# Hybrid decoder block on one core: a new layout of the query columns of the scan's small levels, value columns computed in pairs, meta products in other steps, and one more turn per head

## The chip, the cores and the metric

The kernel runs on one core of a Trainium2 chip. The metric is the device time of one execution in microseconds (us); less is better. Before the change the median of three runs is 873.73 us (872.95 to 874.18).

The engines in the profile: PE is TensorE (matrix products; PEld is its loading of the stationary operand), DVE is VectorE, ACT is ScalarE, POOL is GpSimd, and SP is SyncE, which issues the transfers from device memory (HBM).

## The reference

One layer over 16 meta tokens followed by 512 real tokens, model width 1024, all in float32. Cut to what matters:

```python
u = rmsnorm(h, attn_norm_w)
q, f_raw, i_in, g_out, b_gate, c_gate, x_conv, gate_a, gate_b = split(u @ w_in)   # nine times 1024 columns
q = silu(q);  f = lb + (1 - lb) * sigmoid(f_raw);  k = 1 - f;  v = i_in
o = hgrn2(q, k, v, log f)      # 8 heads of 128: S_t = diag(f_t) S_{t-1} + k_t v_t^T,  o_t = S_t^T q_t
y_a = rmsnorm(o per head) * silu(g_out)
y_b = b_gate * causal_conv3(c_gate * x_conv)
h = h + (sigmoid(gate_a) * y_a + sigmoid(gate_b) * y_b) @ w_out
a, val = split(rmsnorm(h) @ w_up);  h = h + (silu(causal_conv3(a) + b) * val) @ w_down
return rmsnorm(h)[:, 16:]
```

## The kernel before

**Stages.** (1) 0 to about 40 us: loading, the first norm, and the first columns of the input projection (forget gate, query and value of head 0). (2) About 40 to 460 us, called the scan stage here: the rest of the input projection, 128 columns at a time, and between its matmuls the recurrence of the eight heads, one after the other. (3) About 460 to 580 us: output projection and the first six blocks of the FFN. (4) The rest of the FFN and the last norm. The change lies in stage (2).

**Projection.** A float32 product is made of three matmuls in a split format: each operand is cast to a short upper part on ACT, and the lower part is what DVE subtracts from it (L100 and L101 for a single unit, L303 and L304 for a pair). A *single unit* gives one block of 128 output columns for all 528 positions: 8 blocks of the contraction, 3 matmuls each, for each half of the positions, 48 matmuls of 264 columns (`half_unit`, L452). A *pair* gives two such blocks with seven products in place of eight (`Pair`, L343, with `product`, L322): the weights' quarters are first added up on DVE (L313, L314, L318), every product is 4 blocks times 3 matmuls (L330 to L332), and the results are put together from PSUM by a *sink*, a class with four small methods (`FQ`, `CX`, `GA`, `BG`) on DVE and ACT, while ACT copies partial results out (`keep`, L336). A pair loads 1.5 MB of weights (`pair_weights`, L288), a single 0.5 MB. Forget gate with query, conv gate with conv input, output gate with gate a, and b gate with gate b go in pairs; from head 1 on the values are singles, copied by ACT into one tile `V_t` (`value`, L764). The list `items` (L869) gives the order: for each head j the pair FQ of head j+1, the value unit of head j+1, then CX, GA and BG of head j, then the merge.

**Recurrence of a head** (`recur`, L490). It is a generator, and each `yield` ends a step. `tick` (L108) is called after every two contraction blocks of a product; each `beat[1]`-th tick resumes the generator once, so that its small matmuls stand between the large ones. Steps: value transposes; three levels (`LEVELS`: m of 1, 4 and 16 positions in groups of g = 32, 32 and 64); the level of 64; key transposes; state products; output products (L620, L621) with the row norm's statistics; and the last, transposes of the normalised rows (L633) and of the meta rows `om` (L635). What is not done at the head's end is flushed in `merge` (L774). The beat is 6, and 4 for the last head.

**A level** takes blocks of four sub-blocks of m positions. For the sub-blocks of queries that look back on the keys, it lays out six columns' worth of queries in `qv` (L536 to L540), ordered by how many sub-blocks lie between; ACT makes one copy, DVE three products with the decays `T`. Small matmuls of 32 or 64 stationary columns (L544) give the scores in PSUM, DVE then scales the queries in place in three products (L546 to L548) and the keys in one (L556), and three masked copies (L562) put the scores where they belong, by a mask that the host makes.

**Meta products.** Keys of the meta tokens times two queries (L573, 16 stationary columns) stand in the level of 64, in front of its matmuls of 64 stationary columns (L578). Their weighted sum with the values (L611, 2 stationary columns) stands in the step of the state products (L602, L604).

**Order.** Each engine works through its own instructions in a fixed order. That order is made beforehand by a planner that goes by the written order as a priority and by its own estimates of when an operand will be ready; so instructions can stand earlier or later than written. DVE's first products for the next head's level stand far ahead of that head's matmuls in this way.

Of the kernel before, what the change touches and what calls it, by code (L numbers as in the profile page):

```python
# [14 lines left out]
P = 128  # L15
D = 1024
KT = D // P
# [23 lines left out]
SINGLE = [("f", 1), ("q", 1), ("i", 1)] + [u for j in range(1, KT) for u in ([("i", j + 1)] if j + 1 < KT else [])]  # L41
PAIRS = [("g", "ga", 0)]
for _j in range(1, KT):
    PAIRS += ([("f", "q", _j + 1)] if _j + 1 < KT else []) + [("c", "x", _j), ("g", "ga", _j), ("b", "gb", _j)]
# [13 lines left out]
def block_kernel(ctx: ExitStack, tc: tile.TileContext, xT, par, wts, pairs, ident, masks, finw, out):  # L58
# [200 lines left out]
    Vms, Kms, oms = ([const.tile([P, P], F32, name=f"{n}{i}") for i in range(2)] for n in ("Vm", "Km", "om"))  # L259
    ams = [const.tile([P, 2], F32, name=f"am{i}") for i in range(2)]  # L260
# [161 lines left out]
    V_t = p1.tile([P, L + 1], F32, name="V")  # L422
# [6 lines left out]
    nc.gpsimd.memset(V_t[:, L:], 0.0)  # L429
    for i in range(2):  # L430
        nc.gpsimd.memset(Ks[i][:, L:], 0.0)
        nc.gpsimd.memset(Fs[i][:, L:], 1.0)
        nc.gpsimd.memset(As[i], 0.0)
# [28 lines left out]
    with tc.tile_pool(name="rp0", bufs=1) as rp:  # L462
# [22 lines left out]
        raw_unit((h3rd, l3rd), lambda o, at: act.copy(V_t[:, at], o))  # L485
# [4 lines left out]
    def recur(j, oS):  # L490
        b = j % 2
        K, V, F, Q, A = Ks[b], V_t, Fs[b], Qs[b][:, T0:], As[b]
# [27 lines left out]
        for lev, (m, g) in enumerate(LEVELS):  # L520
            ng = SEQ // g
            nb = g // (4 * m)
            lo1, lo2, lo3 = 3 * g // 4, 5 * g // 4, 3 * g // 2
            qv = p2.tile([P, NCH * QW], F32, name="qv", tag="qv").rearrange("p (n w) -> p n w", n=ng)
            q4 = Qm.rearrange("p (n b x) -> p n b x", n=ng, x=4 * m)
            k4 = Km_.rearrange("p (b s m) -> p b s m", s=4, m=m)
            t4 = T.rearrange("p (n b s) -> p n b s", n=ng, s=4)
            tf = T.rearrange("p (b s) -> p b s", s=4)
            v1 = qv[:, :, :lo1].rearrange("p n (b x) -> p n b x", x=3 * m)
            v2 = qv[:, :, lo1:lo2].rearrange("p n (b x) -> p n b x", x=2 * m)  # L530
            v3 = qv[:, :, lo2:].rearrange("p n (b x) -> p n b x", x=m)

            def tb(i):
                return t4[:, :, :, i:i + 1].to_broadcast([P, ng, nb, m])

            act.copy(v1, q4[:, :, :, m:])  # L536
            for i in range(2):
                dve.tensor_tensor(v2[:, :, :, i * m:(i + 1) * m], q4[:, :, :, (2 + i) * m:(3 + i) * m],
                                  tb(1 + i), op=ALU.mult)
            dve.tensor_tensor(v3, v2[:, :, :, m:], tb(1), op=ALU.mult)  # L540
            ps = quarter()
            for n in range(ng):
                r = n * g % P
                pe.matmul(ps[r:r + g, n * g // P, :lo3], K[:, M1 + n * g:M1 + (n + 1) * g], qv[:, n, :],  # L544
                          start=True, stop=True, tile_position=(0, r))
            dve.tensor_tensor(q4[:, :, :, m:2 * m], q4[:, :, :, m:2 * m], tb(0), op=ALU.mult)  # L546
            dve.tensor_tensor(q4[:, :, :, 2 * m:3 * m], v2[:, :, :, :m], tb(0), op=ALU.mult)
            dve.tensor_tensor(q4[:, :, :, 3 * m:], v3, tb(0), op=ALU.mult)  # L548
            n4 = SEQ // (4 * m)
# [7 lines left out]
                              op=ALU.mult)  # L557
            B = Bs[g]
            a4 = B.rearrange("p c (b x) -> p c b x", x=4 * m)
            for r, lo_, hi_ in ((3, 0, lo1), (2, lo1, lo2), (1, lo2, lo3)):  # L560
                mk = mk_t[:, lev, lo_:hi_].rearrange("p (b x) -> p b x", x=r * m)
                dve.copy_predicated(a4[:, :, :, (4 - r) * m:],  # L562
                                    mk.unsqueeze(1).to_broadcast([P, NCH, nb, r * m]),
# [200 lines left out]
    def value(j):  # L764
        return lambda o, at: act.copy(V_t[:, at], o)
# [420 lines left out]
```

## Time and profile before

| | us |
|---|---|
| median of 3 runs | 873.73 |
| the profiled execution | 872.9 |
| its span, first to last instruction | 871.1 |
| TensorE busy | 859.1 (99%) |
| VectorE busy | 717.5 (82%) |
| ScalarE busy | 529.3 (61%) |
| GpSimd busy | 37.5 (4%) |
| granted TensorE clock, mean | 0.998 |

Matmuls overlap in TensorE's pipeline, so the time of one row is longer than the distance between two starts. A line number is that of the kernel before. "Idle before" is how long the engine had nothing to run just ahead of an instruction, with what released it.

### The profile page before, as it was taken

The page shows a single profiled execution, that of the slowest core. Times are in us where ns is not written, and L with a number is a line of the kernel's source. Part 1 is how long each engine was busy: PE and PEld are TensorE (multiplying, and loading weights), DVE is VectorE, ACT ScalarE, POOL GpSimd, SP SyncE. Part 2 cuts the span into 40 slices and gives each one's busy share as a digit, 9 for nine tenths or more (in the row PEclk, how much of TensorE's full clock was granted, in tenths as well). Part 3 has the DMA queues.
Part 4 walks back from the last instruction along what each step waited for, and adds up shares of the span by engine and source line. Part 5 has one row for each costly group of instructions (what it writes and reads, how often), then busy time and mean ns, then how long its engine had stood idle before and what let it go on. Part 6 is the DMA issues. An engine that isn't in the chain of part 4 may idle for free.

```text
span 871.1 us, 17481 instructions
## 1 busy us (share of the span) xinstructions
PE 859.1 (99%) x6996; PEld 814.5 (93%) x6996; DVE 717.5 (82%) x1323; ACT 529.3 (61%) x1004; POOL 37.5 (4%) x110
## 2 busy tenths in 40 slices
PE   8999999999999999999999999999999999999996
PEld 8999999999999999999999999999999999999985
DVE  7899999988989889889986559975877777777766
ACT  7847768676676767776684345554554545545434
POOL 1210110100101001020000000000000000000000
PEclk9999999999999999999999999999999999999999
DMA  7216444343343434434234323533443534433302
GB/s 258 98 50 189 137 142 140 98 147 121 122 146 98 146 109 134 136 102 145 81 112 158 98 73 97 169 100 119 144 147 100 173 116 131 160 97 122 121 25 97
DMA packets 38817, 107.98 MB, mean 124 GB/s; under 512 B 4304, under 2 KB 5712, under 8 KB 38736
## 3 DMA queue, kind: packets, MB, share of 16 engines
q1 hardware_dynamic: 38448, 106.34, 38.4%
q8 instruction: 55, 0.90, 0.4%
q10 hardware_dynamic: 288, 0.52, 0.2%
q14 instruction: 26, 0.21, 0.1%
HBM read 104.75 MB, written 2.10 MB: 123 GB/s over the span
## 4 chain that ended last, share of the span: by engine, by line
PE 80%; DVE 12%; ACT 4%; DMA 3%; issue 1%; SPq 0%; DVEq 0%; ACTq 0%
PE pr L330 14%; PE pr L331 13%; PE pr L332 13%; PE psm L123 4%; PE psm L120 4%; PE psm L121 4%; PE psm L1048 4%; PE psm L1047 4%; PE psm L1046 4%; PE pr L437 3%; DVE wl L304 3%; PE pr L438 3%; PE pr L439 3%; DMA wt<-in_pairs 2%; PE psq L544 1%
## 5 line engine op out<-in xcount | busy, mean ns | idle before, releaser
L330 PE MATMUL pr<-cm,wh 128*128 128x264 f32 (+1 forms) x784 | 227.5, 292 | 0.4 <-ACT c L338 0.2
L331 PE MATMUL pr<-cm,wh 128*128 128x264 f32 (+1 forms) x784 | 222.5, 284 | 0.0
L332 PE MATMUL pr<-cm,wl 128*128 128x264 f32 (+1 forms) x784 | 222.5, 284 | 0.0
L330 PEld LDWEIGHTS pr<-cm,wh 128*128 128x128 f32 x784 | 147.4, 188 | 4.7 <-issue 1.3
L332 PEld LDWEIGHTS pr<-cm,wl 128*128 128x128 f32 x784 | 147.8, 189 | 0.1
L331 PEld LDWEIGHTS pr<-cm,wh 128*128 128x128 f32 x784 | 147.5, 188 | 0.0
L303 ACT CAST wh<-wt 128x1024 fp32r<-128x1024 f32 x88 | 92.2, 1053 | 74.3 <-PE psm L1048 33.9
L304 DVE TENSOR_TENSOR wl<-wt,wh 128x1024 fp32r<-128x1024 f32 x88 | 107.0, 1218 | 30.8 <-ACT wh L303 30.5
L100 ACT CAST wh<-wr 128x1024 fp32r<-128x1024 f32 (+1 forms) x64 | 61.7, 968 | 66.7 <-PE psm L121 31.1
L101 DVE TENSOR_TENSOR wl<-wr,wh 128x1024 fp32r<-128x1024 f32 (+1 forms) x64 | 71.6, 1121 | 37.1 <-ACT wh L100 35.8
L330 PE MATMUL pr<-cf,wh 128*128 128x258 f32 x256 | 72.5, 283 | 0.0
L331 PE MATMUL pr<-cf,wh 128*128 128x258 f32 x256 | 72.1, 282 | 0.0
L332 PE MATMUL pr<-cf,wl 128*128 128x258 f32 x256 | 71.9, 281 | 0.0
L338 ACT COPY c<-pr 128x264 f32<-128x264 f32 (+1 forms) x132 | 49.5, 375 | 33.2 <-PE pr L332 25.8
L304 DVE TENSOR_TENSOR wl<-wr,wh 128x1024 fp32r<-128x1024 f32 x44 | 53.7, 1221 | 11.4 <-ACT wh L303 11.2
L303 ACT CAST wh<-wr 128x1024 fp32r<-128x1024 f32 x44 | 46.2, 1049 | 21.6 <-PE pr L331 19.8
L313 DVE TENSOR_TENSOR wt<-wt 128x1024 f32<-128x1024 f32 x44 | 53.6, 1219 | 3.4 <-DMA wt<-in_pairs 3.3
L330 PE MATMUL pr<-cb,wh 128*128 128x258 f32 x192 | 54.7, 285 | 0.3 <-ACT xr L1007 0.3
L331 PE MATMUL pr<-cb,wh 128*128 128x258 f32 x192 | 54.7, 285 | 0.0
L332 PE MATMUL pr<-cb,wl 128*128 128x258 f32 x192 | 54.4, 283 | 0.0
L331 PEld LDWEIGHTS pr<-cf,wh 128*128 128x128 f32 x256 | 48.6, 190 | 0.8
L330 PEld LDWEIGHTS pr<-cf,wh 128*128 128x128 f32 x256 | 48.1, 188 | 0.7
(304 smaller groups left out, 2247.9 us busy)
## 6 DMA issues: line engine op xcount, KB each, us to landing
wr<-in_wts SPq DMA_DIRECT2D x56, 512.0 KB, 3.7
wr<-in_pairs SPq DMA_DIRECT2D x44, 512.0 KB, 4.2
wt<-in_pairs SPq DMA_DIRECT2D x44, 512.0 KB, 4.0
wt<-in_pairs SPq DMA_DIRECT2D x88, 256.0 KB, 4.8
xt<-in_xT SPq DMA_DIRECT2D x8, 264.0 KB, 4.5
xr<-in_xT SPq DMA_DIRECT2D x8, 264.0 KB, 3.8
out<-zf SPq DMA_DIRECT2D x8, 256.0 KB, 2.3
wr<-in_wts SPq DMA_DIRECT2D x8, 128.0 KB, 4.1
```

Source lines behind the costliest of these rows:

```text
L100: act.copy(h[:, i:i + n, :], raw[:, i:i + n, :])
L101: dve.tensor_tensor(lo[:, i:i + n, :], raw[:, i:i + n, :], h[:, i:i + n, :].bitcast(F32), op=ALU.subtract)
L120: pe.matmul(o, wh, rh[:, a:b], start=first, stop=False)
L121: pe.matmul(o, wh, rl[:, a:b], start=False, stop=False)
L123: pe.matmul(o, wl, rh[:, a:b], start=False, stop=last)
L303: act.copy(h, src)
L304: dve.tensor_tensor(lo, src, h.bitcast(F32), op=ALU.subtract)
L313: dve.tensor_tensor(t[:, 1:3, :], t[:, 1:3, :], t[:, 3:, :].to_broadcast([P, 2, 512]), op=ALU.add)
L330: pe.matmul(ps, h[:, j], ch, start=start and j == 0, stop=False, skip_group_check=True)
L331: pe.matmul(ps, h[:, j], cl, start=False, stop=False, skip_group_check=True)
L332: pe.matmul(ps, lo[:, j], ch, start=False, stop=j == 3, skip_group_check=True)
L338: act.copy(c, r)
```

## The change

- The three `qv` parts get a new order: for each block of four sub-blocks, the six columns of m queries stand together. ACT makes two copies, DVE two products in the place of three. The three that scale the queries in place become one, which reads the first three of the six. The masked copies read runs of 3, 2 and 1 sub-blocks out of each six, and the mask is made accordingly.
- The key products of the meta tokens move into the level with m = 4, behind its matmuls of 32 stationary columns. Their sum gets 64 stationary columns and moves into the level of 64, behind that level's matmuls; ACT's two small operations on its result go with it.
- The values of heads 2 and 3, 4 and 5, 6 and 7 are computed as pairs by a new sink `II`, placed behind FQ of heads 2, 4 and 6; the value tile is doubled. Two small tiles (`Km`, `om`) are no longer doubled.
- One more `yield` in front of the last step, and beats of 6, 5 and 4 (head after an even one, after an odd one, last).

```diff
+    if _j + 1 < KT:
+        PAIRS += [(("f", _j + 1), ("q", _j + 1))]
+        if _j % 2:
+            PAIRS += [(("i", _j + 1), ("i", _j + 2))]
...
+    ams = [const.tile([P, 64], F32, name=f"am{i}") for i in range(2)]
...
-            act.copy(v1, q4[:, :, :, m:])
-            for i in range(2):
-                dve.tensor_tensor(v2[:, :, :, i * m:(i + 1) * m], q4[:, :, :, (2 + i) * m:(3 + i) * m],
-                                  tb(1 + i), op=ALU.mult)
-            dve.tensor_tensor(v3, v2[:, :, :, m:], tb(1), op=ALU.mult)
+            act.copy(qs[:, :, 0], q4[:, :, 1])
+            act.copy(qs[:, :, 3::2], q4[:, :, 2:])
+            dve.tensor_tensor(qs[:, :, 1:5:3], q4[:, :, 2:], tf[:, :, 1:3].unsqueeze(3).to_broadcast([P, n4, 2, m]),
+                              op=ALU.mult)
+            dve.tensor_tensor(qs[:, :, 2], qs[:, :, 4], tf[:, :, 1:2].to_broadcast([P, n4, m]), op=ALU.mult)
...
-            dve.tensor_tensor(q4[:, :, :, m:2 * m], q4[:, :, :, m:2 * m], tb(0), op=ALU.mult)
-            dve.tensor_tensor(q4[:, :, :, 2 * m:3 * m], v2[:, :, :, :m], tb(0), op=ALU.mult)
-            dve.tensor_tensor(q4[:, :, :, 3 * m:], v3, tb(0), op=ALU.mult)
+            dve.tensor_tensor(q4[:, :, 1:], qs[:, :, :3], tf[:, :, :1].unsqueeze(3).to_broadcast([P, n4, 3, m]),
+                              op=ALU.mult)
...
+            if m == 4:
+                pma = pmisc.tile([P, 512], F32, name="pm", tag="pm")
+                for i in range(2):
+                    pe.matmul(pma[:16, 2 * i:2 * i + 2], KM[:, i, :], Q[:, 14 - T0:16 - T0], start=True, stop=True)
+                am = ams[b]
+                act.copy(am[:16, :2], pma[:16, 0:4:3])
...
+            for k, a, e in ((0, 0, 3 * m), (1, 3 * m, 5 * m), (2, 5 * m, 6 * m)):
+                dve.copy_predicated(a4[:, :, :, (k + 1) * m:],
+                                    mk[:, :, a:e].unsqueeze(1).to_broadcast([P, NCH, nb, e - a]), got[:, :, :, a:e])
...
-        pma = pmisc.tile([P, 512], F32, name="pm", tag="pm")
-        for i in range(2):
-            pe.matmul(pma[:16, 2 * i:2 * i + 2], KM[:, i, :], Q[:, 14 - T0:16 - T0], start=True, stop=True)
...
+        pms = pmisc.tile([P, 512], F32, name="pm", tag="pm")
+        pe.matmul(pms[:64, :P], am, Vm, start=True, stop=True)
...
-        pe.matmul(pms[:2, :P], am, Vm, start=True, stop=True)
...
         yield
+        yield
         ps = quarter()
         for c in range(NCH):
             pe.transpose(ps[:, c, :], on[:, c, :], id_t)
...
+    class II:
+        def __init__(self, j):
+            self.v1, self.v2 = Vs[j % 2], Vs[(j + 1) % 2]
+        def n1a(self, r2, c1):
+            dve.tensor_tensor(self.v1[:, lo_], r2, c1, op=ALU.add)
+        def n2b(self, r3, c3):
+            minus(self.v2[:, hi_], r3, c3)
+        def n2a(self, r1):
+            act.activation(self.v2[:, lo_], r1, AF.Copy, scale=-1.0)
+        def n1b(self, r3, c2):
+            dve.tensor_tensor(self.v1[:, hi_], r3, c2, op=ALU.add)
...
-            items += [("p", lambda j=j: FQ(j + 1)), ("s", value(j + 1))]
+            items += [("p", lambda j=j: FQ(j + 1))] + ([("p", lambda j=j: II(j + 1))] if j % 2 else [])
...
-                beat[:] = [0, 6 if arg + 2 < KT else 4]
+                beat[:] = [0, 4 if arg + 2 == KT else 5 if arg % 2 else 6]
```

## Rows read from the trace of the kernel before

**Rows 1.** The page: the chain that ended last, shares of the span.

```profile
PE 80%; DVE 12%; ACT 4%; DMA 3%; issue 1%; SPq 0%; DVEq 0%; ACTq 0%
```

**Rows 2.** Busy us by stretch: PE, PEld, DVE, ACT, POOL; clock; DMA; heads 1-6.

```profile
91.10:149.20 58.10, 57.17 (x532) 55.08 (x531) 56.63 (x123) 42.08 (x90) 6.45 (x10) 1.00 0.43 130
149.20:203.90 54.70, 54.70 (x519) 53.22 (x518) 49.60 (x110) 38.33 (x82) 2.97 (x10) 1.00 0.43 135
203.90:258.80 54.90, 54.83 (x519) 53.19 (x518) 49.13 (x105) 38.35 (x82) 2.98 (x10) 1.00 0.41 126
...
sum 331.80, PE 329.84 PEld 319.76 DVE 301.02 ACT 234.75 POOL 24.21; mean PE 54.97 PEld 53.29 DVE 50.17 ACT 39.12 POOL 4.04
```

**Rows 3.** The same view: head 0's stretch.

```profile
40.00:91.10 51.10, 50.83 (x484) 49.14 (x483) 50.44 (x117) 33.39 (x77) 4.98 (x10) 1.00 0.37 114
```

**Rows 4.** Timeline of PE: start, duration, engine, line; large matmuls.

```profile
204.81 0.28 PE L330 MATMUL pr<-cm,wh 128*128 128x264 f32 x1
...
207.25 0.28 PE L332 MATMUL pr<-cm,wl 128*128 128x264 f32 x1
```

**Rows 5.** Groups by line and shape: DVE's weight work (busy us, mean ns).

```profile
L304 DVE TENSOR_TENSOR wl<-wt,wh 128x1024 fp32r<-128x1024 f32 x88 | 107.0, 1218 | 30.8 <-ACT wh L303 30.5
L101 DVE TENSOR_TENSOR wl<-wr,wh 128x1024 fp32r<-128x1024 f32 x56 | 68.4, 1222 | 37.1 <-ACT wh L100 35.8
L313 DVE TENSOR_TENSOR wt<-wt 128x1024 f32<-128x1024 f32 x44 | 53.6, 1219 | 3.4 <-DMA wt<-in_pairs 3.3
L314 DVE TENSOR_TENSOR wt<-wt,wr 128x512 f32<-128x512 f32 x44 | 30.0, 684 | 2.3 <-DMA wr<-in_pairs 2.2
```

**Rows 6.** The same view: DVE's small operations in the recurrence.

```profile
L556 DVE TENSOR_TENSOR K<-K,TK 128x384 f32<-128x384 f32 x24 | 13.3, 553 | 0.1
L538 DVE TENSOR_TENSOR qv<-Q,T 128x128 f32<-128x128 f32 x32 | 8.4, 284 | 0.0
L538 DVE TENSOR_TENSOR qv<-Q,F 128x128 f32<-128x128 f32 x16 | 5.9, 394 | 6.1 <-ACT F L651 6.1
L562 DVE COPY_PREDICATED B<-mk_t,psq 128x96 f32<-128x96 int32 x16 | 4.4, 277 | 0.0
L583 DVE TENSOR_TENSOR Q<-Q,T 128x256 f32<-128x256 f32 x8 | 3.4, 419 | 0.9 <-PE psq L578 0.9
```

**Rows 7.** Timeline of PE: meta products of head 1 and their neighbours.

```profile
113.60 0.25 PE L573 MATMUL pm<-Q,KM 128*16 128x2 f32 x4
113.78 0.45 PE L578 MATMUL psq<-Q,K 128*64 128x64 f32 x8
...
123.65 0.83 PE L604 MATMUL psq<-Vt,Kt 128*128 128x128 f32 x6
124.41 0.38 PE L611 MATMUL pm<-Vm,am 128*2 128x128 f32 x2
124.72 0.39 PE L330 MATMUL pr<-cm,wh 128*128 128x264 f32 x1
```

**Rows 8.** Waits of PE and PEld: who for whom, us in total, times, longest.

```profile
PE pm L635 <- DVE om L629: 1.2, 3, 0.6
PE psq L633 <- ACT on L628: 0.7, 1, 0.7
...
PEld pm L635 <- DVE om L629: 2.4, 5, 0.9
...
PEld psq L633 <- ACT on L628: 1.0, 1, 1.0
```

**Rows 9.** Timeline of PE: head 5's output products and its last step.

```profile
349.67 0.38 PE L620 MATMUL po<-S,Q 128*128 128x128 f32 x2
...
360.59 0.38 PE L635 MATMUL pm<-id_t,om 128*128 128x2 f32 x2 [0.64 <-DVE om L629]
```

**Rows 10.** Waits of DVE and of ACT from 149.2 to 422.9 us.

```profile
DVE wl L304 <- ACT wh L303: 9.4, 11, 1.4
...
ACT wh L303 <- PE pr L331: 23.3, 38, 0.9
```

## Prediction before the run

> **What bounds the kernel now.** I read four views in this order: the chain of waits, the busy time by stretch, the engine's own order of instructions in one head, and the waits. The chain that ended last is 80% TensorE, 12% VectorE [rows 1]. The change lies wholly in the scan stage, in which eight heads follow each other, so I cut that stage at each head's first transposes. In the six windows of heads 1 to 6 TensorE is busy 329.84 of 331.8 us and VectorE 301.02; in window 1 VectorE is busy 56.63 of 58.1 us, in window 2 49.60 of 54.7, in window 3 49.13 of 54.9 [rows 2], and in head 0's 50.44 of 51.1 [rows 3]. The clock column stands at 1.00 in all of them, the 2.4 GHz level. A busy TensorE proves nothing by itself, since its instructions overlap; the distance of their starts does: 21 matmuls of 264 columns start between 204.81 and 207.25, so one costs 0.122 us of TensorE's time, not the 0.28 of its row [rows 4]. Nothing waits in such a stretch. So TensorE's stream of matmuls sets the pace, and VectorE, at 91% of the six windows and 99% of head 0's, stands close behind it. The reader should see two engines, of which the change relieves the first and loads the second.
>
> **Value pairs.** Six single value units become three pairs. Two singles are 2 x 48 = 96 matmuls of 264 columns, a pair is 7 products x 4 blocks x 3 = 84. Removed: 3 x 12 = 36 matmuls x 0.122 = **4.4 us** on the bounding engine [rows 4]. This term is firm as long as TensorE sets the pace. In windows 1, 3 and 5 TensorE gets 84 - 48 = 36 matmuls more (4.4 us), in 2, 4 and 6 it loses 48 (5.9 us).
>
> VectorE pays for it. Each pair makes 3.5 lower parts of a 1024-element block (3.5 x 1.218 = 4.3), one 1024 sum (1.22), two 512 sums (2 x 0.684 = 1.4) and three sinks of 264 elements (nearest row 0.419, so 1.3): 8.2 us [rows 5, 6]. Two singles made two lower parts, 2 x 1.222 = 2.4, and ScalarE copied their values out. So +5.8 us a pair, **+17.3 us** of VectorE in all, in windows 1, 3 and 5. ScalarE makes 1.5 more casts a pair, three keeps and one sink in place of four copies: under 2 us more a pair if a cast costs no more than VectorE's subtraction of the same size. It is busy 42.08 of 58.1 us in window 1, 38.33 of 54.7 in window 2, and ends no stretch; I cost it at nothing. What hides it is that idle quarter. If that cover were gone its casts would come late to VectorE, and that belongs to the VectorE rival below. SyncE issues 1.5 MB for a pair where 1.0 MB went for two singles; the transfers take 43% of the DMA engines in window 1 [rows 2], and even in the windows that get shorter the 6 MB of four pairs remain near that share. I cost that at nothing; a late transfer would show as VectorE's first sum waiting.
>
> **Three operations in the levels.** Before, six VectorE products of 128 elements a level: in the two levels with m of 4 and 16 six x 0.284 = 1.70 us, in the level with m of 1, which reads single elements 16 bytes apart, six x at least 0.394 = 2.36 us. After: one of 256 elements (0.419), one of 128 (0.284), one of 384 (0.553) = 1.26 us for m of 4 and 16, a gain of 0.45 each [rows 6]. For m of 1 no row has the new layout. Low end: only the single-element one pays, 0.42 + 0.39 + 0.55 = 1.37. High end: all are stretched by 394/284, 0.58 + 0.39 + 0.77 = 1.74. I take the low end for the 384 one, since the 384 row stays at 0.553 over all three levels although its level of m 1 also has runs of three in steps of four, and 0.50 for the 256 one, in the middle: 1.45, a gain of 0.9. The masked copies now read their scores in interrupted runs; six a head at 0.277 could stretch by the same factor, 0.65 us, or by nothing; they wrote interrupted runs before, so I take 0.2. Net per head 0.45 x 2 + 0.9 - 0.2 = **1.6 us less VectorE**, between 0.9 and 1.9; over eight heads 12.8 us. None of it lies on the path while TensorE paces, so it counts at zero in the sum: it pays for the pairs. ScalarE gets a second copy a level, hidden as above.
>
> The Trainium skill, page "SBUF — State Buffer", section "Door 1: The DMA port swizzle", says that fp32 data come in lines of 16 bytes and that an access wants at least two hits on each line to run at full rate. By it the 256 operation, which takes two neighbours of every four, is unpenalised (0.42 rather than 0.50) and the 128 one is not, and the head gains 1.7 instead of 1.6. The trace bears the penalty out (394 against 284 ns); the exemption no run before the change shows. The terms here don't use it.
>
> **VectorE's account.** Windows 1 to 6: 301.0 + 17.3 - 6 x 1.6 = 308.7 us. TensorE's: 331.8 less 4.4 and the six heads' part of the two terms below, about 2.7, = 324.7. So VectorE goes from 91% to 95%. In head 0's window it ran at 99% and TensorE was still busy 50.83 of 51.1 [rows 3], in window 1 at 97% with 0.93 lost, in windows 2 and 3 with 0.0 and 0.07 [rows 2]. Between 0 and 0.9 us a window I take 0.17, nearer to the many quiet ones: **+1.0 us** of new waits of TensorE.
>
> **Meta products.** Two small products change the column width of the array between two large matmuls. The sum's product has two stationary columns: from its predecessor's last start (123.65 + 5 x 0.11 = 124.20) to the next large matmul at 124.72 pass 0.52 us, where the plain step would take 0.11. Moved behind the 64-column products at 64 columns of its own, it adds two starts at 0.11 [rows 7]. 0.52 - 0.11 - 0.22 = 0.19 saved. The key products take 0.18 from 113.60 to 113.78 in front of the 64-column products; behind 32-column ones they cost four starts of about 0.025, so 0.08 saved. 0.27 x 8 = **2.1 us**. Low end -0.8: the planner places large matmuls between the moved products and their neighbours, so that they still switch, on both sides. High end 2.4. The added wait, the sum's product on ScalarE's copy of the key products, lies two steps behind its producer; behind it on TensorE would stand the pair's next product.
>
> **One more turn.** TensorE waits 1.2 and 0.7 us for the normalised rows, its weight loads 2.4 and 1.0 us for the same [rows 8]: ends of the gain 1.9 and 3.4 us if all goes, and zero if none does. In head 5 the wait ends at 360.59, 10.9 us after the step before began at 349.67 [rows 9]. That step has 16 starts at 0.11 (1.8 us), and six ticks of six matmuls are 4.4 us: written order alone gives 6.2, so the planner had already put the last step 4.7 us later. One turn more makes the written place 10.6 us (beat 6), 9.1 (beat 5) or 7.6 (last head, beat 4), so mostly where it is now, and the wait is only partly covered. I take **1.5 us**. Ten resumptions need 60, 50 and 40 ticks of 70, 56 and 42, so only head 0's last one falls into the merge, where its input has long been there: nothing. Single buffers for two small tiles and the second value buffer add no wait, since the heads run one after the other.
>
> **Sum.** Against the profiled execution (872.9 us, span 871.1): 872.9 - 4.4 - 2.1 - 1.5 + 1.0 = 865.9. The median of the runs is 873.7, 0.8 higher: **866.7 us** predicted, its own range 863 to 869. Beyond the scan the code is the same.
>
> **Rivals.** (a) The small steps give nothing: the planner separates the moved products and the normalised rows are as late as before. For it, the planner's own placing above; against it, key products and 64-column products stand side by side now [rows 7]. 872.9 - 4.4 + 1.0 + 0.8 = 870.3.
> (b) VectorE becomes the bound and the kernel is slower. Its idle time in the six windows is 30.8 us, 5.1 a window. If that is waiting for ScalarE that no pressure removes (lower parts waited 9.4 us for their casts), the windows grow to 308.7 + 30.8 = 339.5 us, 7.7 more than now: 881.4. It decides from an idle of (331.8 - 308.7)/6 = 3.9 us a window; below that the kernel is faster. Against it: the casts themselves waited 23.3 us for TensorE to give up weight buffers, so the idle is mostly TensorE's pace handed on [rows 10], and head 0 shows 0.7 idle.
> (c) The same, half: idle falls to 3.3 us a window. 308.7 + 19.8 = 328.5 against 324.7: 3.8 us on top of the forecast, less the 1.0 taken there, about 869.5.
> (d) All small terms at their high ends without new waits: 872.9 - 4.4 - 2.4 - 3.4 + 0.8 = 863.5.
>
> **Chances.** Forecast 0.53, (a) 0.14, (c) 0.13, (d) 0.11, (b) 0.09. The range goes from 862 to 872, which leaves out (b) and some of the tails. A measurement of this kernel can tell 0.2%, 1.7 us, from no change: "within" is 872.0 to 875.4, reached by (b) in a mild form and the tail of (a) and (c), 0.07; slower 0.08, the rest of (b) and its neighbours; faster 0.85.
>
> **What would show it.** Pairs: 36 large matmuls fewer, and windows of some 60, 49, 59, 49 us. Levels: three VectorE products a level at 0.42, 0.28 and 0.55 us for m of 4 and 16. Meta: the sum's product directly behind the 64-column products, no start distance of 0.2 around it. Turn: TensorE's waits for the normalised rows under 0.5 us. VectorE: 309 us over six windows; if it stands at 99% and TensorE's starts of large matmuls show gaps behind lower parts, (b) or (c) holds. The prediction is wrong if the kernel is not faster, or if the gain comes from outside the scan.

## The result, and the profile after

The changed kernel takes 866.62 us (median of 4 runs, 866.15 to 867.39) against 873.70 us for the kernel before in the same comparison (4 runs, 872.95 to 874.18): a ratio of 0.992 with an interval of 0.9905 to 0.9935, 7.1 us less. The forecast was 866.7 us. The profiled execution took 866.84 us with a span of 865.1 us, where before it was 872.9 and 871.1. The part behind the scan is unchanged (411.4 to 411.6 us from the first output-projection matmul to the end in both), so all of the gain lies in the scan stage.

The chain that ended last, on the page of the changed kernel:

```profile
PE 86%; DVE 7%; DMA 3%; ACT 2%; issue 1%; SPq 0%; DVEq 0%; ACTq 0%
```

TensorE has 86% of it instead of 80%, VectorE 7% instead of 12% [rows 1], although VectorE now has more to do. Next the busy time by stretch, cut at each head's first transposes as before (columns as in [rows 2]):

```profile
91.30:151.30 60.00, 60.00 (x562) 58.50 (x561) 59.24 (x118) 44.51 (x99) 5.15 (x10) 1.00 0.46 144
151.30:201.40 50.10, 49.89 (x478) 48.16 (x477) 48.67 (x98) 37.65 (x84) 5.48 (x10) 1.00 0.42 131
201.40:259.80 58.40, 58.40 (x550) 56.96 (x549) 53.41 (x108) 41.85 (x92) 5.17 (x10) 1.00 0.43 131
259.80:310.00 50.20, 49.68 (x478) 48.13 (x477) 47.03 (x95) 37.46 (x84) 4.82 (x10) 1.00 0.43 132
...
sum 325.80, PE 324.43 PEld 315.31 DVE 307.66 ACT 238.18 POOL 29.47; mean PE 54.07 PEld 52.55 DVE 51.28 ACT 39.70 POOL 4.91
```

The windows alternate, 60.0, 50.1, 58.4, 50.2 us, where 60, 49, 59, 49 were forecast. The six together are 325.8 us, 6.0 less than 331.8 [rows 2]; head 0's window is 51.3, practically as before (51.1) [rows 3]. VectorE's sum is 307.66 (308.7 forecast), 94% of the windows. The clock column still reads 1.00.

The groups by line show what the pairs added and what the levels saved on VectorE (columns as in [rows 5]; the scaling lines L534, L536 and L542 take the place of L538's six):

```profile
L308 DVE TENSOR_TENSOR wl<-wt,wh 128x1024 fp32r<-128x1024 f32 x94 | 114.3, 1220 | 26.3 <-ACT wh L307 26.0
L317 DVE TENSOR_TENSOR wt<-wt 128x1024 f32<-128x1024 f32 x47 | 57.3, 1220 | 8.2 <-DMA wt<-in_pairs 8.2
L322 DVE TENSOR_TENSOR s<-wt,wr 128x512 f32<-128x512 f32 x47 | 32.2, 686 | 0.5
...
L542 DVE TENSOR_TENSOR Q<-qv,T 128x384 f32<-128x384 f32 x16 | 8.9, 554 | 0.0
L534 DVE TENSOR_TENSOR qv<-Q,T 128x256 f32<-128x256 f32 x16 | 6.7, 417 | 0.1
L536 DVE TENSOR_TENSOR qv<-qv,T 128x128 f32<-128x128 f32 x16 | 4.5, 282 | 0.0
L563 DVE COPY_PREDICATED B<-mk_t,psq 128x96 f32<-128x96 int32 x16 | 4.5, 279 | 0.0
L542 DVE TENSOR_TENSOR Q<-qv,F 128x384 f32<-128x384 f32 x8 | 4.4, 550 | 0.0
L534 DVE TENSOR_TENSOR qv<-Q,F 128x256 f32<-128x256 f32 x8 | 4.1, 511 | 0.0
L536 DVE TENSOR_TENSOR qv<-qv,F 128x128 f32<-128x128 f32 x8 | 3.3, 407 | 0.0
```

Sums are 47 instead of 44, at unchanged durations [rows 5]. For m of 4 and 16 a level's three operations take 0.417 + 0.282 + 0.554 = 1.25 us, for m of 1 0.511 + 0.407 + 0.550 = 1.47.

The meta products in TensorE's timeline of head 2 (start, duration, engine, line):

```profile
159.86 0.55 PE L540 MATMUL psq<-qv,K 128*32 128x48 f32 x32
160.22 0.24 PE L555 MATMUL pm<-Q,KM 128*16 128x2 f32 x4
160.40 0.39 PE L334 MATMUL pr<-cm,wh 128*128 128x264 f32 x1
...
168.65 0.29 PE L336 MATMUL pr<-cm,wl 128*128 128x264 f32 x1
168.87 0.45 PE L575 MATMUL psq<-Q,K 128*64 128x64 f32 x8
169.15 0.38 PE L578 MATMUL pm<-Vm,am 128*64 128x128 f32 x2
169.47 0.39 PE L334 MATMUL pr<-cm,wh 128*128 128x264 f32 x1
...
177.45 0.83 PE L606 MATMUL psq<-Vt,Kt 128*128 128x128 f32 x6
178.04 0.37 PE L334 MATMUL pr<-cm,wh 128*128 128x264 f32 x1
```

Both moved products stand directly behind products of a near or equal width: the key products (16 stationary columns) behind those of 32, the sum's product (64) behind those of 64. Behind the state products the next large matmul now follows without the two-column product between them, compare [rows 7]. The last steps of heads 3 and 4, and the waits of the whole run (who, for whom; us in total, times, longest):

```profile
237.03 0.38 PE L615 MATMUL po<-S,Q 128*128 128x128 f32 x2
...
247.78 0.60 PE L629 MATMUL psq<-id_t,on 128*128 128x128 f32 x4
248.22 0.28 PE L631 MATMUL pm<-id_t,om 128*128 128x2 f32 x2
...
290.40 0.38 PE L615 MATMUL po<-S,Q 128*128 128x128 f32 x2
...
299.86 0.33 PE L629 MATMUL psq<-id_t,on 128*128 128x128 f32 x1 [0.30 <-ACT on L623]
300.40 0.38 PE L631 MATMUL pm<-id_t,om 128*128 128x2 f32 x2 [0.22 <-DVE om L624]
```

```profile
PE pm L631 <- DVE om L624: 1.6, 4, 0.6
...
PE psq L629 <- ACT on L623: 0.5, 2, 0.3
...
PEld pm L631 <- DVE om L624: 2.1, 4, 0.8
...
PEld psq L629 <- ACT on L623: 1.3, 3, 0.5
```

In head 3 the last step starts 10.75 us after the output products and waits for nothing; in head 4 it starts 9.46 us after them and waits twice. In total these waits are 2.1 us for TensorE where [rows 8] had 1.9: they did not fall.

**An account of starts.** To see where each term went I added up TensorE's time in the scan stage by distances of starts. A cluster of small matmuls costs the distance between the large matmuls around it, less the 0.122 us of one. What two neighbouring large matmuls are apart beyond 0.122, with nothing between them, I call a gap; a record missing from the trace counts as one too. In e1, e3, e8 and e12 the last head's four transposes stand behind the last projection matmul; there the 1.13 or 1.14 us up to the first output-projection matmul are in its last step. All in us; "clusters" are the 64-column, meta and state products, "VectorE" is its busy time from 91 to 450 us, and "e" numbers are the experiments below.

| kernel | median | ratio to before (95%) | profiled | clusters | last steps | gaps | VectorE |
|---|---|---|---|---|---|---|---|
| before | 873.7 | 1 | 872.9 | 15.66 | 8.86 | 7.31 | 324.7 |
| after | 866.62 | 0.992 (0.9905–0.9935) | 866.84 | 12.66 | 9.26 | 8.16 | 337.4 |
| e1 single values | 869.54 | 0.9958 (0.9944–0.9973) | 872.21 | 12.46 | 6.88 | 11.58 | 316.8 |
| e2 pairs only | 871.68 | 0.9984 (0.9972–0.9996) | 872.95 | 15.61 | 9.05 | 9.69 | 340.9 |
| e3 no turn | 868.40 | 0.994 (0.9926–0.9954) | 870.26 | 12.65 | 7.83 | 11.06 | 336.3 |
| e4 meta back | 871.41 | 0.997 (0.9959–0.998) | 872.0 | 15.91 | 6.78 | 13.02 | 332.6 |
| e5 old levels | 869.96 | 0.9965 (0.9951–0.9979) | 874.18 | 12.68 | 10.95 | 12.58 | 340.4 |
| e6 om on ScalarE | 866.78 | 0.9928 (0.9916–0.994) | 866.78 | 12.65 | 6.72 | 11.00 | 335.9 |
| e7 later last | 869.29 | 0.9954 (0.9941–0.9967) | 869.36 | 12.47 | 8.47 | 10.76 | 336.1 |
| e8 sum on GpSimd | 889.98 | 1.0187 (1.0167–1.0206) | 889.1 | 12.49 | 9.74 | 28.07 | 330.5 |
| e9 two sums there | 901.62 | 1.0318 (1.0297–1.0339) | 902.1 | 13.86 | 21.78 | 25.58 | 329.4 |
| e10 turn in odd heads | 867.42 | 0.9925 (0.9911–0.9939) | 866.91 | 12.66 | 8.89 | 8.12 | 337.8 |
| e11 e8 and e6 | 882.34 | 1.0096 (1.0082–1.011) | 882.34 | 12.47 | 7.70 | 24.25 | 334.0 |
| e12 sum left out | 874.01 | 1.0003 (0.9994–1.0012) | 877.5 | 12.48 | 6.89 | 20.06 | 312.4 |

Each row is one profiled execution; those of e1, e3, e5 and e12 are 2 to 4 us above their medians, so their gaps are too large by up to that much. Some 5 us of most rows of gaps (4.5 to 7.5) are not waiting but missing records: before, 52 distances are one matmul too long, after, 49. What goes beyond such a distance adds up to 0.8 us before and 1.1 after. "VectorE" is read in a window of fixed length, and in a slower kernel less of the stage lies in it. The ratios compare with runs of the kernel before beside each experiment, whose median lay between 873.3 and 874.3 us, so a difference of two medians below carries some 0.6 us. From before to after: 36 large matmuls less, -4.4; clusters -3.0; the level products, 16.83 to 16.96, +0.1; last steps +0.4; gaps +0.85. Sum -6.1, and the stage went from 429.57 to 423.43 us, also -6.1.

### The profile page after: what moved, and what is told of

It reads as the page before. It is cut to its first block, busy times and chain, and to the rows that moved or that the text cites. A ratio compares the mean times of both kernels' runs of the same rounds, so it can differ in the third digit from the quotient of the medians.

```text
span 865.1 us, 17393 instructions
## 1 busy us (share of the span) xinstructions
PE 853.6 (99%) x6960; PEld 810.0 (94%) x6960; DVE 723.5 (84%) x1275; ACT 535.2 (62%) x1034; POOL 43.1 (5%) x109
## 4 chain that ended last, share of the span: by engine, by line
PE 86%; DVE 7%; DMA 3%; ACT 2%; issue 1%; SPq 0%; DVEq 0%; ACTq 0%
PE pr L334 17%; PE pr L335 16%; PE pr L336 16%; PE psm L127 4%; PE psm L124 4%; PE psm L125 4%; PE psm L1062 4%; PE psm L1061 4%; PE psm L1060 4%; DMA wt<-in_pairs 2%; PE pr L441 2%; PE pr L442 2%; PE pr L443 2%; DVE wl L308 2%; PE psq L540 2%
## 5 line engine op out<-in xcount | busy, mean ns | idle before, releaser
L334 PE MATMUL pr<-cm,wh 128*128 128x264 f32 (+1 forms) x868 | 253.9, 293 | 0.1
L335 PE MATMUL pr<-cm,wh 128*128 128x264 f32 (+1 forms) x868 | 246.3, 284 | 0.0
L336 PE MATMUL pr<-cm,wl 128*128 128x264 f32 (+1 forms) x868 | 244.9, 283 | 0.0
L334 PEld LDWEIGHTS pr<-cm,wh 128*128 128x128 f32 x868 | 163.3, 188 | 5.2 <-ACT c L342 1.5
L336 PEld LDWEIGHTS pr<-cm,wl 128*128 128x128 f32 x868 | 163.4, 189 | 0.0
L335 PEld LDWEIGHTS pr<-cm,wh 128*128 128x128 f32 x868 | 163.3, 188 | 0.0
L307 ACT CAST wh<-wt 128x1024 fp32r<-128x1024 f32 x94 | 98.0, 1049 | 70.8 <-PE psm L1062 31.3
L308 DVE TENSOR_TENSOR wl<-wt,wh 128x1024 fp32r<-128x1024 f32 x94 | 114.3, 1220 | 26.3 <-ACT wh L307 26.0
L104 ACT CAST wh<-wr 128x1024 fp32r<-128x1024 f32 (+1 forms) x58 | 55.5, 960 | 65.5 <-PE psm L125 31.1
L105 DVE TENSOR_TENSOR wl<-wr,wh 128x1024 fp32r<-128x1024 f32 (+1 forms) x58 | 64.3, 1112 | 30.5 <-ACT wh L104 29.3
L308 DVE TENSOR_TENSOR wl<-wr,wh 128x1024 fp32r<-128x1024 f32 x47 | 57.4, 1221 | 9.4 <-ACT wh L307 9.4
L317 DVE TENSOR_TENSOR wt<-wt 128x1024 f32<-128x1024 f32 x47 | 57.3, 1220 | 8.2 <-DMA wt<-in_pairs 8.2
```

Source lines behind the costliest of these rows:

```text
L104: act.copy(h[:, i:i + n, :], raw[:, i:i + n, :])
L105: dve.tensor_tensor(lo[:, i:i + n, :], raw[:, i:i + n, :], h[:, i:i + n, :].bitcast(F32), op=ALU.subtract)
L307: act.copy(h, src)
L308: dve.tensor_tensor(lo, src, h.bitcast(F32), op=ALU.subtract)
L317: dve.tensor_tensor(t[:, 1:3, :], t[:, 1:3, :], t[:, 3:, :].to_broadcast([P, 2, 512]), op=ALU.add)
L334: pe.matmul(ps, h[:, j], ch, start=start and j == 0, stop=False, skip_group_check=True)
```

## The experiments

The first runs undo one part each. Two theories run through them. P: TensorE's path sets the time and each part is worth its own matmuls and waits, whatever VectorE has to do. V: VectorE's load decides how much of that arrives.

**e1, values single again**, all else as in the changed kernel:

```diff
-SINGLE = [("f", 1), ("q", 1), ("i", 1)]
+SINGLE = [("f", 1), ("q", 1), ("i", 1)] + [u for j in range(1, KT) for u in ([("i", j + 1)] if j + 1 < KT else [])]
-        if _j % 2:
-            PAIRS += [(("i", _j + 1), ("i", _j + 2))]
-            items += [("p", lambda j=j: FQ(j + 1))] + ([("p", lambda j=j: II(j + 1))] if j % 2 else [])
+            items += [("p", lambda j=j: FQ(j + 1)), ("s", value(j + 1))]
-                beat[:] = [0, 4 if arg + 2 == KT else 5 if arg % 2 else 6]
+                beat[:] = [0, 6 if arg + 2 < KT else 4]
```

> The changed kernel with the six values as single units again (beats 6 and 4), all else as changed. Theory P, TensorE paces: 36 large matmuls come back, +4.4 us, and the new gaps between large matmuls (0.7) go, so 3.7 to 4.4 above the changed kernel: 870.3 to 871.0. Theory V, VectorE holds TensorE back: with 17.3 us less VectorE work most of the matmuls' time is won back: under 868.5.

869.54 us, 2.9 more than the changed kernel: between the two. It has the 36 matmuls back (4.4 us), its last steps cost 2.4 less, and its gaps 3.4 more. The last steps of heads 2, 4 and 6, with a beat of 6 here, start 10.6 to 11.7 us after the output products and cost 0.73 to 1.10. The place of its largest wait is new, for ScalarE's copies out of PSUM:

```profile
PE pr L332 <- ACT c L340: 3.6, 6, 1.0
```

**e2, the pairs alone**: the kernel before, with the new lists, the class II, two value buffers, the single buffers of `Km` and `om`, and the beats of 6, 5 and 4.

```diff
-PAIRS = [("g", "ga", 0)]
+PAIRS = [(("g", 0), ("ga", 0))]
...
+        if _j % 2:
+            PAIRS += [(("i", _j + 1), ("i", _j + 2))]
...
-                beat[:] = [0, 6 if arg + 2 < KT else 4]
+                beat[:] = [0, 4 if arg + 2 == KT else 5 if arg % 2 else 6]
```

> The kernel before with nothing but the value pairs (and their beats 6, 5, 4). Theory P: 873.7 - 4.4 + about 1 = 869.5 to 870.5, although VectorE now has 318 us of work in the six windows of 327. Theory V: without the levels' relief VectorE becomes the bound, TensorE waits 4 us or more: 873 or above.

871.68 us: only 2.0 under the kernel before, between the two ranges. The pairs alone, without what relieves VectorE and TensorE, bring a little less than half of their 4.4. Gaps took 2.4 (7.31 to 9.69).

**e3, without the turn:**

```diff
         yield
-        yield
         ps = quarter()
```

> The changed kernel without the extra turn. Theory D, the distance from the output products to the last step sets the wait: heads 1, 3, 5 and 7 get waits again, 2 to 3 us, and heads 2, 4 and 6 wait no less: 868.5 to 870. Theory N, the planner puts the last step where it believes its input ready, whatever is written: within 0.5 us of the changed kernel's 866.6.

868.40 us, 1.8 more: that the turn does nothing falls. But it doesn't work as I thought, and theory D's mechanism falls too: without it the last steps cost less, 7.83 against 9.26, and the gaps 2.9 more (in an execution 1.9 us above the median). Head 4's output products and last step in this run:

```profile
294.31 0.38 PE L615 MATMUL po<-S,Q 128*128 128x128 f32 x2
...
304.35 0.35 PE L630 MATMUL pm<-id_t,om 128*128 128x2 f32 x2
```

Without the turn that step starts 10.04 us after the output products and waits for nothing, where the changed kernel, with the turn, starts it at 9.46 and waits twice.

**e4, meta products at their old places** and in their old widths:

```diff
-            if m == 4:
-                pma = pmisc.tile([P, 512], F32, name="pm", tag="pm")
...
+        pma = pmisc.tile([P, 512], F32, name="pm", tag="pm")
+        for i in range(2):
+            pe.matmul(pma[:16, 2 * i:2 * i + 2], KM[:, i, :], Q[:, 14 - T0:16 - T0], start=True, stop=True)
...
-        pe.matmul(pms[:64, :P], am, Vm, start=True, stop=True)
...
+        pe.matmul(pms[:2, :P], am, Vm, start=True, stop=True)
```

> The changed kernel with the meta products in their old steps and 2 stationary columns. Theory P, every start distance on TensorE counts: 0.37 us a head back, +2.9 us: 869.2 to 869.8; the clusters of small matmuls show 1.95 us a head for the two steps in place of 1.58. Rival, the column switches hide in waits that are there anyway: under 867.5.

871.41 us, 4.8 more, above both ranges. The clusters themselves take 3.25 more and the level products 0.3 less, together the 2.9 of theory P. The last steps cost 2.5 less and the gaps 4.9 more, of which two gaps behind late weights make 3.6. Around the first of them, the timeline:

```profile
251.85 1.23 DVE L317 TENSOR_TENSOR wt<-wt 128x1024 f32<-128x1024 f32 x1 [3.13 <-DMA wt<-in_pairs]
...
253.94 0.28 PE L335 MATMUL pr<-cm,wh 128*128 128x264 f32 x1
...
255.81 0.39 PE L336 MATMUL pr<-cm,wl 128*128 128x264 f32 x1 [1.60 <-DVE wl L308]
```

A block of weights lands late, and VectorE's first sum waits 3.13 us for it. The lower part that TensorE needs next stands behind that sum in VectorE's order and starts at 254.54, and TensorE's next large matmul starts 1.87 us after the one before it. In the whole stage VectorE waits longer for that transfer than in the changed kernel (from 91 to 450 us 9.5 us in 5 waits, longest 3.2; there 5.0 in 5, longest 1.2).

**e5, the levels in their old form** (six products of 128 elements, the old layout of columns and masks):

```diff
-            dve.tensor_tensor(qs[:, :, 1:5:3], q4[:, :, 2:], tf[:, :, 1:3].unsqueeze(3).to_broadcast([P, n4, 2, m]),
-                              op=ALU.mult)
-            dve.tensor_tensor(qs[:, :, 2], qs[:, :, 4], tf[:, :, 1:2].to_broadcast([P, n4, m]), op=ALU.mult)
+            for i in range(2):
+                dve.tensor_tensor(v2[:, :, :, i * m:(i + 1) * m], q4[:, :, :, (2 + i) * m:(3 + i) * m],
+                                  tb(1 + i), op=ALU.mult)
+            dve.tensor_tensor(v3, v2[:, :, :, m:], tb(1), op=ALU.mult)
```

> The changed kernel with the old layout of the query columns (six VectorE products a level in place of three), all else as changed. VectorE gets 1.6 us a head more, 317 of some 326 us in the six windows, 97%. Theory P: TensorE still paces, 0 to 1.5 us above the changed kernel: 866.6 to 868.1. Theory V: VectorE is the bound from there on, 3 us or more above: 869.6 and up; then the layout is what lets the pairs pay.

869.96 us, 3.3 more, in theory V's range (its runs spread from 867.95 to 874.18). It gives TensorE no matmul more, so P alone doesn't explain it. The layout is worth 3.3 us here. That it is worth them as cover of the pairs is not shown: no run has the layout without the pairs, the planner's order changed with the edit, and the pairs are worth 2.0 us without the layout and the rest (e2) and 2.9 with them (e1), 0.9 more. The profiled execution has a further loss:

```profile
92.17 0.38 PE L641 MATMUL pm<-id_t,om 128*128 128x2 f32 x2 [2.18 <-DVE om L634]
...
93.30:96.70 3.40, 3.40 (x18) 3.33 (x17) 3.40 (x6) 2.00 (x6) 0.00 (x0) 0.50 0.15 22
```

After TensorE had waited 2.18 us for head 0's meta rows, the granted clock fell to 0.50, the 1.2 GHz level, from 93.3 to 96.7 us; only 18 matmuls lie in that stretch. So a part of this row's gaps is the clock. The profiles of e8, e9, e11 and e12 have such stretches in the scan stage too; the changed kernel's has none.

Undone one by one, the four parts are worth 2.9 + 4.8 + 1.8 + 3.3 = 12.8 us, and together 7.1: not a sum of independent terms. The next runs look for what makes the waits move.

**e6, the meta row scaled on ScalarE** instead of VectorE, which takes the wait for om out of VectorE's queue:

```diff
-        dve.tensor_scalar(om[:2], om[:2], rs[:2, NCH:], None, op0=ALU.mult)
+        act.activation(om[:2], om[:2], AF.Copy, scale=rs[:2, NCH:])
```

> The changed kernel with the scaling of the two meta rows on ScalarE, right behind the scaling of the token rows, in place of VectorE. Theory Q, these rows come late because they queue behind weight work on VectorE: the waits of TensorE for them (1.6 us, four times, and their weight loads 2.1) go for the most part: 864.5 to 865.5. Rival, the whole chain from the row norm is late, and the last step waits for the token rows instead: 866.0 to 867.0.

866.78 us, the same, in the rival's range. Yet the last steps did fall, by 2.54, and the gaps rose by 2.84. Its waits between 30 and 460 us name the new places (in the changed kernel the first of them is 1.5 us in 7 waits, and the others are under 0.5):

```profile
PEld pr L334 <- ACT c L342: 3.3, 11, 0.7
...
PE pr L336 <- DVE wl L308: 0.8, 1, 0.8
...
PE pr L334 <- ACT c L342: 0.6, 2, 0.5
```

**e7, the last step of the heads with beat 5 written a turn later**, and head 0 set to beat 5:

```diff
         yield
+        if j % 2 == 0:
+            yield
...
-            beat[:] = [-4, 6]
+            beat[:] = [-4, 5]
```

> The changed kernel with a second extra turn for heads 0, 2, 4 and 6, and a beat of 5 for head 0, so that their last step stands 15 ticks behind the output products. Theory D, the distance sets the wait: the last steps of these heads cost 0.58 us each as those of heads 1, 3 and 5 do, 3.7 us less: 862.9 to 864. Rival, VectorE's load in the shorter windows sets it: the waits move along with the step, 866 to 867.5.

869.29 us, 2.7 more: a miss for both expectations. In heads 4 and 6 the last step still starts 9.3 us after the output products, as before the edit: the planner pulled it forward again. The written place isn't the placed one. In head 2 it starts 10.9 us after them, as before, and now costs 0.58; in head 0 it costs 1.63.

**e10, the turn in odd heads only:**

```diff
         yield
-        yield
+        if j % 2:
+            yield
         ps = quarter()
```

> The changed kernel with the extra turn for heads 1, 3, 5 and 7 only, where its trace shows the last step without waits (0.58 us each); heads 2, 4 and 6 had 0.66 to 0.77 without the turn in the kernel before and 1.28 to 1.72 with it. Theory D, the distance sets each head's wait: 2.5 us less, 864.0 to 864.5. Theory C, what one place gives another takes: 866 to 868.

867.42 us, theory C's range, and the same as with the turn in every head. What one last step costs, head by head (worked out as in the account):

| head | 0 | 1 | 2 | 3 | 4 | 5 | 6 | 7 |
|---|---|---|---|---|---|---|---|---|
| before | 0.58 | 2.06 | 0.68 | 0.85 | 0.77 | 1.40 | 0.66 | 1.86 |
| after | 1.43 | 0.57 | 1.28 | 0.58 | 1.59 | 0.58 | 1.72 | 1.51 |
| e10 | 1.56 | 0.57 | 1.02 | 0.58 | 1.50 | 0.57 | 1.59 | 1.50 |
| e3, no turn | 1.60 | 0.91 | 1.22 | 0.61 | 0.72 | 0.61 | 0.72 | 1.40 |
| e4, meta back | 1.16 | 0.57 | 1.00 | 0.57 | 0.66 | 0.57 | 0.66 | 1.56 |

0.57 is a last step that waits for nothing. Heads 3 and 5 come down to it with the turn, but without it (e3) they are at 0.61 already. In heads 4 and 6 the last step is placed 9.4 us after the output products in the changed kernel and in e10, and om is there at 9.9 to 10.1. Neither their own turn (e10 has none there) nor the beat of 5 explains this place: e3 without any turn and e4 with it have the same beats, place the step at 9.95 to 10.05, and it costs 0.66 to 0.72 there. The planner's place for a head depends on the whole order, and what tips it, no run tells. In head 0 om is ready 11.5 us after the output products, where it was ready at 9.8 before. With om's scaling on ScalarE (e6) head 0 costs 0.50, so the step waits for VectorE there; why VectorE comes to it later, no run tells.

**e8, e9, e11: VectorE relieved by GpSimd.** e8 moves the last of a scan pair's weight sums, e9 also the one before it, e11 is e8 with the edit of e6.

```diff
-        dve.tensor_tensor(s4f, t[:, 3, :], xf[:, 0, :], op=ALU.add)
+        (nc.gpsimd if next_pair[0] <= len(PAIRS) else dve).tensor_tensor(s4f, t[:, 3, :], xf[:, 0, :], op=ALU.add)
```

> The changed kernel with the last weight sum of each pair of the scan stage (512 elements, 0.68 us on VectorE, 31 pairs) on GpSimd, which is idle there 9 parts in 10. Theory C, the waits that are left on TensorE (some 5 us) are set by VectorE's total load and only change their place when an edit of the order moves one of them: with 21 us less on VectorE most of them go, 862 to 864.5. Theory L, they are latencies of the row norm's chain and the planner's places for it: 866 to 867.5. If GpSimd takes over 3 us for one sum and the two share a port, VectorE's other operations get longer and it is slower.

> The same with both 512-element sums on GpSimd, which then follow each other there, 42 us less on VectorE. Theory C: at or under the run with one sum, 861 to 863.5. Theory L: 866 to 867.5. A third outcome, the chain of two sums on a slow engine makes the last products' weights late: above 868, with TensorE waiting for a lower part.

> One sum on GpSimd and the meta rows' scaling on ScalarE. Theory C: with VectorE's load lower the two gains add, as they could not with the load as it was: 861 to 863.5. Theory L: 866 to 867.

889.98, 901.62 and 882.34 us: all slower than the kernel before. The groups of e8 show why it is no test of VectorE's load:

```profile
L550 DVE TENSOR_TENSOR K<-K,TK 128x384 f32<-128x384 f32 x24 | 17.9, 745 | 0.3 <-PE psq L540 0.3
L534 DVE TENSOR_TENSOR qv<-Q,T 128x256 f32<-128x256 f32 x16 | 10.0, 623 | 0.1
L548 DVE TENSOR_TENSOR TK<-F,TK 128x128 f32<-128x128 f32 x8 | 7.3, 917 | 0.0
```

One of the sums and the operation that meets it, in the timeline of e8:

```profile
94.25 1.63 POOL L322 TENSOR_TENSOR s<-wt,wr 128x512 f32<-128x512 f32 x1 [5.28 <-issue]
94.63 1.44 DVE L548 TENSOR_TENSOR TK<-F,TK 128x128 f32<-128x128 f32 x1
```

A sum on GpSimd takes 1.93 us on average (31 of them, 60.0 us, 1.28 to 4.85) against 0.69 on VectorE, and VectorE's operations get longer on average: L550 745 ns instead of 558, L534 623 instead of 417, L548 917 instead of 382. These means mix two kinds. The 19 of L550 that meet no GpSimd sum take 558 ns, the five that do 1.32 to 1.66 us. Of the 61 VectorE operations that begin while a sum runs, 31 take 0.74 to 1.17 us longer than in the changed kernel, and each of them ends after that sum, by 0.02 to 1.1 us, as the one above does; the other 30 keep their time to 0.02 us. That e11 takes back 7.6 us of e8 with an edit that alone gave nothing (e6) shows once more that the parts don't add.

**e12, that sum left out** of the scan pairs, so that VectorE has less to do and nothing else takes it over:

```diff
-        dve.tensor_tensor(s4f, t[:, 3, :], xf[:, 0, :], op=ALU.add)
+        if next_pair[0] <= len(PAIRS):
+            s4 = blocks(3, 4)
+        else:
+            dve.tensor_tensor(s4f, t[:, 3, :], xf[:, 0, :], op=ALU.add)
```

> The changed kernel with the last weight sum of each pair of the scan stage left out: the operand before it is used in its place, so the projection is a different one, with the same matmuls. VectorE has 0.68 us a pair less, 21 us in the stage, and no other engine has more. Theory C, VectorE's total load sets the 5 us of waits that are left on TensorE: 861.5 to 864. Theory L, they come from the length of the row norm's chain and the places the planner gives the last step: 865.5 to 867.5, with the last steps of heads 2, 4 and 6 still at 1.0 us or more.

874.01 us, 7.4 more and above both ranges, though VectorE is busy 312.4 of 359 us instead of 337.4. Its waits between 91 and 450 us:

```profile
DVE wt L317 <- DMA wt<-in_pairs: 17.2, 13, 3.2
...
PEld pr L337 <- DVE za L654: 5.3, 3, 2.7
PE pr L337 <- DVE za L654: 4.7, 3, 2.5
```

The part that is read in place of the sum lies in the weight tile itself, which by the code is so held until the last cast and subtraction have read it, and VectorE waits 17.2 us for the transfers into it instead of 5.0. So the edit adds a wait of its own, and it is no clean test of VectorE's load: 25 us less of it came together with more waiting for weights.

## Why the prediction was right

**Pairs: right on the path, and conditional.** -4.4 forecast, and the account from before to after closes with -4.4 (the other terms leave -6.1 - (-3.0 + 0.1 + 0.4 + 0.85) = -4.4). The windows and VectorE's 307.66 us came within 1.2 us each of the forecast. That the pairs alone bring 2.0 (e2), and 2.9 when they alone are undone (e1), was not in my sum.

**Meta products: the mechanism right, the size too small.** 2.1 forecast, 3.0 less in the clusters, 2.9 with the levels' +0.1; above my high end of 2.4. Going back costs 3.25 in the clusters (e4). From the first state product to the next large matmul pass 0.59 us (177.45 to 178.04) where [rows 7] had 1.07: 0.48 less, where I had counted 0.52 - 0.11 = 0.41. That is 8 x 0.07 = 0.6 of the 0.9 missing: the plain step that I left standing behind the state products is not 0.11 but 0.03 (0.59 less five starts at 0.11). Rival (a), that the planner would part the moved products from their neighbours, did not come.

**Levels: right, with a price I had not given.** The operations took 1.25 and 1.47 us (1.26 and 1.45 forecast), and the masked copies did not stretch, 279 against 277 ns, where I had set 0.2 us a head aside. The six before at m of 1 had taken 2.44 and not 2.36, so VectorE gains 0.45 x 2 + 0.97 = 1.9 us a head instead of 1.6. "It counts at zero in the sum" holds in the sum and not in the kernel: without it 3.3 us of the gain are gone (e5). The operation that takes two neighbours of every four at m of 1 took 511 ns against 417 with longer runs, near the 0.50 that I had taken. The sentence that I drew from the Trainium skill, page "SBUF — State Buffer", section "Door 1: The DMA port swizzle", that two hits on each line leave it unpenalised, is not settled by this. I had looked only at what it reads: it also writes, at m of 1, single elements 12 bytes apart (columns 1 and 4 of each six), and no run separates the two.

**One more turn: the step that failed.** I wrote that TensorE's waits for the normalised rows would fall by 1.5 us and end under 0.5. They are 2.1 us, after 1.9. I had worked out the written place for each beat and took it to be "mostly where it is now". But the planner doesn't keep the written place: without the turn (e3) it put the last steps of heads 4 and 6 10.04 us after the output products, where they waited for nothing, and in the changed kernel 9.4 us, before the rows were there. So all the rest of the change took the last steps from 8.86 to 7.83, and the turn brought them to 9.26: it costs 1.4 us there, where I had counted a gain of 1.5. The turn has a value all the same, 1.8 us (e3), and by e10 the turn in the odd heads alone does as well; but it shows up as fewer gaps elsewhere, not as shorter last steps.

**New waits: right as far as the account can tell.** +1.0 forecast, +0.85 in gaps, of which only 0.3 lies in distances longer than a missing record leaves. Rival (b), VectorE as the bound, falls: the kernel is faster, and with VectorE at 99% of window 1 TensorE was busy all of it, without a gap beyond a missing record. Over all runs VectorE's load doesn't order the times: e1 with 317 and e12 with 312 us are slower than the changed kernel with 337, though each carries a burden of its own (36 matmuls, later weights).

The sum came out because errors cancelled in part: +0.4 instead of -1.5 in the last steps, -2.9 instead of -2.1 in the meta products. That leaves -6.1 against the forecast -7.0 in profiled executions. The medians lie 7.1 apart, since the profiled execution before was 0.8 under its median and the one after 0.2 above. So that forecast and median agree to 0.1 us is luck; the mechanism earns the sign and most of the size.

**What stays open.** Some 5 to 8 us of waiting (last steps beyond 0.57 a head, and the long gaps) move from place to place with every edit: e1, e3, e4 and e6 have last steps 1.4 to 2.5 us cheaper and gaps 2.8 to 4.9 us dearer. The runs show three places where they turn up: ScalarE's copies out of PSUM (e1, e6), late weight transfers (e4, e12), and the last steps. Which of these would give way if the planner's order were held fixed, no run here tells, for every edit changed that order too. No version tried beats the changed kernel; e6 and e10 equal it.

## What to carry to other kernels

Where one engine paces, take the work that a change removes from it as a firm term by distances of starts, not by durations, and then look at what the other engines must do for it: relief that counts at zero by itself can be worth as much as a term of the sum (3.3 us here). In a kernel whose order a planner writes, a wait removed at one place is worth only what the sum of all gaps says, so compare the whole stage, not the place. Undoing parts one by one gives each part's worth in company, and these don't add up.

## What the runs showed of the hardware

- Sums on GpSimd (fp32, two operands of 512 elements) and VectorE's work held each other up. A VectorE operation running when such a sum ended could take 0.74 to 1.17 us longer: 5 elements (1.12 us instead of 0.16), strided 128 (L548, 1.44 to 1.46 instead of 0.38), and plain subtractions of 512 (1.45 to 1.47 instead of 0.69) or 1024 (2.0 to 2.3 instead of 1.22) alike. In the other cases the VectorE operation kept its time, and the longest sums on GpSimd, 2.2 to 4.85 us where the shortest take 1.28, met such operations. The expectation of e8 had tied this to sums of over 3 us; it came with sums of 1.93 on average.
- At m of 1, the product of 256 fp32 elements that reads pairs of neighbours 16 bytes from pair to pair, and writes single elements 12 bytes apart, took 511 ns against 417 with longer runs. Which of the two costs is not shown.
- After a long wait of TensorE the granted clock could fall to the 1.2 GHz level inside the stage (e5, 93.3 to 96.7 us, after a wait of 2.18), so that a wait cost more than its own length.
- Masked copies that read PSUM in runs of three, two and one of six took no longer than those that read it in one run (279 and 277 ns).
